# A two-layer decoder trunk on one core: layer 0's mixer with the norm's sums earlier, another order of products, table loads in the planner, and a gate by tanh

## The chip, the cores and the metric

The kernel runs on one core of a Trainium2 chip. A core has five engines, each with its own queue that it works through in order: TensorE (PE; its weight loads are listed as PEld), VectorE (DVE), ScalarE (ACT), GpSimd (POOL) and SyncE (SP), which here only issues transfers. The metric is the device time of one execution in microseconds (us); lower is better. A run's time is that of the whole program; its span goes from the first to the last instruction that the profiler recorded.

## The reference

512 tokens of width 1024 pass through two layers, all in float32. Each layer is a half-step SwiGLU, a mixer and another half-step SwiGLU, each behind an RMS norm. The change lies in the mixer of layer 0:

```
def hybrid_mixer(h, w_in, conv_w, ...):                       # h = rms_norm(x, gain)
    z, xbc, dt_raw, qm, km, vm, om, ig, fg = split_cols(h @ w_in, HY_SPLITS)
    xbc = silu(causal_dwconv(xbc, conv_w, conv_b))            # four taps
    xs, bm, cm = split_cols(xbc, ...)
    y = ssd_chunked(xs, softplus(dt_raw + dt_bias), -exp(a_log), bm, cm, 128) + xs * d_skip
    y = rms_norm(y * silu(z), ssd_norm)                       # in two groups
    hm = mlstm_chunked(qm, km, vm, ig + igate_bias, fg + fgate_bias, 128)
    hm = rms_norm(hm, mlstm_norm) * sigmoid(om)               # the output gate
    return concatenate([y, hm]) @ w_out
```

`ssd_chunked` and `mlstm_chunked` are recurrences over four chunks of 128 tokens, with exponentials of sums of gates.

## The kernel before

**Precision.** Every large product is made of three: a float32 operand is split into a high and a low part ("form"), and high x high, high x low and low x high are added up (`mm3`, lines 235 to 237). The high part is a copy on ScalarE, the low part a difference on VectorE (`parts`, L355 and L357). A form that the code calls `summed` is made otherwise: ScalarE writes the negative (L385), a transfer issued by GpSimd adds the raw weights (L386), ScalarE writes the high part (L387). That spares VectorE and loads the DMA.

**Seven products for eight.** A block of the mixer's input product (512 columns of the weights, called a unit here) is computed by a Strassen-like scheme: seven products of quarters, named A11, A12, A22, S1 to S4 after the form of the features that they use, each 8 x 3 = 24 matrix instructions of 256 columns. Differences of weights are made on VectorE (`less`, L350 on 1024 elements). `product_seven` issues the seven; three of the accumulator banks (tag "hm", four in turn) take them: A holds A11, S2, S3 and A22, B holds A12, D holds S1 and S4. Between two products in one bank the running sum is read out by ScalarE (`keep`, L778) or VectorE (`c11` to `c22`, L350 and L821).

**The mixer's order.** `hybrid` lays down: a small product for the gates (`gates`), which then also issues the norm's sums of squares and reciprocal roots (`settle_later`, twice: L321 on TensorE, a VectorE step L618, a power on GpSimd L620; then L330 on TensorE and a copy on ScalarE L624 that makes the row "rrow") and some fifty tiny operations on the gates; a first unit without the scheme (`unit_eight`, 96 instructions of 512 columns), which needs no scaled features because it is scaled after; the features' seven forms (`xforms`, L438, L350, L355, L357), which need "rrow"; then the units X0, X1 (with a four-tap convolution each, L1034), Z0, Z1, Q, K, V0, V1, O0, O1; the SSD (`ssd`), its gating (`gated`), the mLSTM (`mlstm`) and the output product. The output gate's sigmoid is applied to "og" by ScalarE as O0 and O1 are read out (L824 and L831), and multiplied in L1399. SSD, gating and mLSTM need Exp and Silu on ScalarE.

**What sets the order.** Nothing is issued as it is written. `Plan.add` records each step with its engine, an estimated time, and what it reads and writes; `Plan.order` then schedules the whole program as a list: at each point the step that can start first goes next, among equals the one with the smallest due time (the longest estimated way to the end). TensorE's steps keep their written order within each of several streams ("filler", "ssd", "mlstm"). Buffers are limited by `BUFS` and the `bufs` of each tile: four weight forms in the mixer, four raw weight blocks, two "hu" tiles (the output of the first unit and of X0 and X1, which the convolution reads). The estimate of a ScalarE step knows nothing of function tables, which are loaded (ACT_TABLE_LOAD) when a function needs another table than the one that is in.

## Time and profile before

| | us |
|---|---|
| median of 3 runs | 2032.71 |
| lowest, highest | 2028.99, 2040.58 |
| the profiled execution: its time | 2027.85 |
| its span | 2026.1 |
| TensorE busy in the span | 1963.7 |
| VectorE, ScalarE, GpSimd busy | 1629.9, 1289.5, 321.5 |

In the profile, L12 is line 12 of the kernel; a group is named by its line, engine, operation, and the tiles it writes and reads. A wait is put down to what ended last before it. Busy shares are averages over stages that have different limits, so the mixer, from about 345 to 780 us of the span, is read in stretches. A stretch's granted clock is the share of its full clock that TensorE was given; 0.50 is half speed. The built program has 30 table loads on ScalarE.

### The profile page before, as it was taken

How to read it: one execution, taken by the hardware profiler on the slowest of the kernel's cores; microseconds unless marked ns; L12 is line 12 of the kernel's file. 1: busy time of each engine (PE TensorE's matmuls, PEld its weight loads, DVE VectorE, ACT ScalarE, POOL GpSimd, SP SyncE). 2: the span in 40 equal slices, each digit the busy share in tenths (PEclk: the TensorE clock that was granted, in tenths of full speed). 3: DMA queues.
4: the chain of work that ended last, by engine and by line, in shares of the span. 5: the costliest groups of instructions: out<-in, count | busy, mean ns of one | idle time of the engine just before them, and what ended most of it. 6: DMA issues, size and time to landing. Idle time of an engine off the chain costs nothing.

```text
span 2026.1 us, 36431 instructions
## 1 busy us (share of the span) xinstructions
PE 1963.7 (97%) x14674; PEld 1816.1 (90%) x14674; DVE 1629.9 (80%) x2373; ACT 1289.5 (64%) x1924; POOL 321.5 (16%) x401
## 2 busy tenths in 40 slices
PE   8999999889998999999999999999999999999998
PEld 6999998789997788999999899999966578999998
DVE  6888888798587657989888898979778747988886
ACT  6666666468678753757566566757656834756665
POOL 1000011212124120101012000101323521100010
PEclk9999999999999999999999999999999999999999
DMA  7566666357867442666565366666745202566664
GB/s 219 136 163 154 163 161 166 104 148 180 208 178 218 106 118 64 155 158 167 146 166 149 87 161 173 159 158 157 192 105 103 65 1 84 141 164 160 161 164 118
DMA packets 226609, 292.89 MB, mean 145 GB/s; under 512 B 15036, under 2 KB 196488, under 8 KB 225928
## 3 DMA queue, kind: packets, MB, share of 16 engines
q1 hardware_dynamic: 200728, 199.30, 31.7%
q0 software_dynamic: 25632, 91.24, 24.2%
q8 instruction: 115, 1.88, 0.4%
q14 instruction: 54, 0.44, 0.1%
q10 hardware_dynamic: 80, 0.02, 0.0%
HBM read 192.96 MB, written 6.33 MB: 98 GB/s over the span
## 4 chain that ended last, share of the span: by engine, by line
PE 62%; DVE 6%; ACT 5%; DMA 4%; issue 4%; POOL 1%; ACTq 0%; POOLq 0%; DVEq 0%; SPq 0%
PE pA L236 7%; PE pA L235 7%; PE pA L237 7%; PE pD L235 3%; PE pD L237 3%; PE pD L236 3%; PE hm L235 3%; PE hm L236 3%; PE hm L237 3%; DMA form<-raw 2%; PE pB L235 2%; PE pB L237 2%; PE pB L236 2%; DMA raw<-in_ffn_w_gate 1%; DVE raw L350 1%
## 5 line engine op out<-in xcount | busy, mean ns | idle before, releaser
L357 DVE TENSOR_TENSOR form<-raw,form 128x1024 fp32r<-128x1024 f32 (+2 forms) x382 | 456.3, 1199 | 119.8 <-ACT form L355 118.5
L355 ACT ACTIVATE form<-raw 128x1024 fp32r<-128x1024 f32 (+1 forms) x382 | 392.1, 1030 | 208.2 <-DVE raw L350 138.0
L386 POOL DMA_DIRECT2D form<-raw x172 | 150.9, 879 | 1370.7 <-ACT form L385 1325.2
L350 DVE TENSOR_TENSOR raw<-raw 128x1024 f32<-128x1024 f32 (+2 forms) x281 | 333.1, 1190 | 27.3 <-DMA raw<-in_ffn_w_up 10.7
L235 PE MATMUL pA<-xf,form 128*128 128x256 f32 x1152 | 321.3, 279 | 0.0
L237 PE MATMUL pA<-xf,form 128*128 128x256 f32 x1152 | 320.8, 278 | 0.0
L236 PE MATMUL pA<-xf,form 128*128 128x256 f32 x1152 | 320.7, 278 | 0.0
L385 ACT ACTIVATE form<-raw 128x1024 fp32r<-128x1024 f32 (+1 forms) x172 | 178.1, 1036 | 164.0 <-PE pD L237 70.9
L235 PEld LDWEIGHTS pA<-xf,form 128*128 128x128 f32 x1152 | 217.2, 189 | 0.4
L237 PEld LDWEIGHTS pA<-xf,form 128*128 128x128 f32 x1152 | 217.3, 189 | 0.0
L236 PEld LDWEIGHTS pA<-xf,form 128*128 128x128 f32 x1152 | 217.0, 188 | 0.2
L236 PE MATMUL pA<-hid,form 128*128 128x256 f32 x704 | 198.1, 281 | 4.0 <-DVE hid L357 4.0
L235 PE MATMUL pA<-hid,form 128*128 128x256 f32 x704 | 198.2, 282 | 1.0 <-ACT hid L355 0.9
L237 PE MATMUL pA<-hid,form 128*128 128x256 f32 x704 | 197.0, 280 | 0.0
L387 ACT ACTIVATE form<-raw 128x1024 fp32r<-128x1024 f32 (+1 forms) x172 | 176.3, 1027 | 0.0
L235 PE MATMUL pD<-xf,form 128*128 128x256 f32 x576 | 160.3, 278 | 0.0
L237 PE MATMUL pD<-xf,form 128*128 128x256 f32 x576 | 160.2, 278 | 0.0
L236 PE MATMUL pD<-xf,form 128*128 128x256 f32 x576 | 160.2, 278 | 0.0
L350 DVE TENSOR_TENSOR ft<-ft 128x256 f32<-128x256 f32 (+2 forms) x296 | 151.9, 544 | 5.4 <-ACT ft L604 1.9
L236 PEld LDWEIGHTS pA<-hid,form 128*128 128x128 f32 x704 | 132.4, 188 | 6.0 <-DVE hid L357 6.0
L235 PEld LDWEIGHTS pA<-hid,form 128*128 128x128 f32 x704 | 132.6, 188 | 2.3 <-ACT hid L355 1.5
L237 PEld LDWEIGHTS pA<-hid,form 128*128 128x128 f32 x704 | 132.6, 188 | 0.0
(447 smaller groups left out, 5397.5 us busy)
## 6 DMA issues: line engine op xcount, KB each, us to landing
form<-raw POOLq DMA_DIRECT2D x156, 512.0 KB, 5.6
raw<-in_ffn_w_gate SPq DMA_DIRECT2D x88, 512.0 KB, 4.1
raw<-in_ffn_w_up SPq DMA_DIRECT2D x88, 512.0 KB, 3.7
raw<-in_ffn_w_down SPq DMA_DIRECT2D x64, 512.0 KB, 4.1
raw<-in_hy_w_in SPq DMA_DIRECT2D x44, 512.0 KB, 4.5
raw<-in_ffn_w_down SPq DMA_DIRECT2D x32, 384.0 KB, 3.5
raw<-in_hy_w_out SPq DMA_DIRECT2D x16, 512.0 KB, 3.5
form<-raw POOLq DMA_DIRECT2D x16, 384.0 KB, 4.5
```

The costliest lines, as they stand in the source:

```text
L235: mm(out, l[0], r[0], start=start, stop=False)
L236: mm(out, l[0], r[1], start=False, stop=False)
L237: mm(out, l[1], r[0], start=False, stop=stop)
L350: (self.p if pool else self.v)(n, lambda: e.tensor_tensor(out(), x(), y(), op=op), reads, writes)
L355: self.s(n, lambda: nc.scalar.activation(hi(), src(), AF.Copy), srck, hik)
L357: n, lambda: nc.vector.tensor_tensor(lo(), src(), hi().bitcast(F32), op=ALU.subtract), srck + hik, lok
L385: self.s(n, lambda: nc.scalar.activation(f()[:, 1], raw, AF.Copy, scale=-1.0), rawk, lok)
L386: self.plan.add("gpsimd", 0.85, lambda: nc.gpsimd.dma_start(f()[:, 1], raw, accum_op=ALU.add), rawk + lok, lok, 5.5)
L387: self.s(n, lambda: nc.scalar.activation(f()[:, 0], raw, AF.Copy), rawk, hik)
```

## The change

Four things; the third is in the planner, which orders the whole program, the others are in layer 0's mixer.

1. The norm's sums and rows are taken out of `gates`, which becomes a generator, and issued in `unit_eight` between its first blocks' products. The gates' tiny operations are recorded after the unit's products.
2. `product_seven` issues A11, S1, S2, A12, S3, S4, A22 in place of A11, A12, S1, S2, S4, S3, A22. In the last eight units the summed forms are A12, S4, A22 in place of A12, S2, S4. "hu" has three buffers for two.
3. The planner keeps the table that is loaded: a step that needs another gets 8 us added to its due time (`PATIENCE`), and, once chosen, 1.28 us to its start (`TABLE`). Steps with Silu, Exp and Sin name their table.
4. The output gate is 0.5 * (1 + tanh(om / 2)): ScalarE applies Tanh with scale 0.5, L1399's product becomes (og + 1) * h, and the 0.5 goes into the row factor of the norm (L1419).

```diff
-    LAG = 0.25
+    LAG, TABLE, PATIENCE = 0.25, 1.28, 8.0
...
-        start, free = [None] * n, {e: 0.0 for e, _ in queue}
+        start, free, loaded = [None] * n, {e: 0.0 for e, _ in queue}, None
+        change = lambda i: self.steps[i][7] not in (None, loaded)
...
-                    c = [(max(free[e], known[i]), due[i] + self.steps[i][6], i) for i in q[:most] if known[i] is not None]
+                    c = [
+                        (max(free[e], known[i]), due[i] + self.steps[i][6] + self.PATIENCE * change(i), i)
+                        for i in q[:most] if known[i] is not None
+                    ]
...
-            free[e] = t + self.steps[i][1]
+            if change(i):
+                loaded, start[i] = self.steps[i][7], t + self.TABLE
+            free[e] = start[i] + self.steps[i][1]
...
         keep(kept[0], A)
         self.part_done = [len(self.plan.steps) - 1]
-        B = self.bank("hm")
-        mul(B, b21, self.A12, True)
-        c11(pairs, B)
         D = self.bank("hm")
         mul(D, less(b11, b12, b11), self.S1, True)
         keep(kept[2], D)
         mul(A, less(t2, b22, b11), self.S2, False)
         keep(kept[1], A)
+        B = self.bank("hm")
+        mul(B, b21, self.A12, True)
+        c11(pairs, B)
+        mul(A, less(b12, b22, b12), self.S3, False)
+        c22(pairs, A)
         mul(D, b22, self.S4, False)
         c12(pairs, D)
-        mul(A, less(b12, b22, b12), self.S3, False)
-        c22(pairs, A)
         mul(A, less(t2, b21, t2), self.A22, False)
         c21(pairs, A)
...
                 if func:
-                    self.s(T, lambda: act(o(), o(), func), ok, ok)
+                    self.s(T, lambda: act(o(), o(), func, scale=0.5), ok, ok)
...
         for qs in ((0, 1), (3, 2)):
             for i in range(4):
+                if i in (1, 2):
+                    self.settle_later()
...
-        self.gates(w, g)
+        gates = self.gates(w, g)
+        next(gates)
...
-        self.conv(self.unit_eight(self.columns(w, X0 + 1024), "hu", 2), 8, bc)
+        u = self.unit_eight(self.columns(w, X0 + 1024), "hu", 3)
+        next(gates)
+        self.conv(u, 8, bc)
...
-        many = dict(summed=(self.A12, self.S2, self.S4))
+        many = dict(summed=(self.A12, self.S4, self.A22))
...
-        og = rows(O0, "og", 256, AF.Sigmoid)
+        og = rows(O0, "og", 256, AF.Tanh)
...
+        yield
         plan.stream = "ssd"
-        self.settle_later()
-        self.settle_later()
...
-                self.v(256, lambda ps=ps, h=h, c=c: tt(ox(c, h), ox(c, h), ps()[:, 0:256], op=ALU.mult), [psk, ok(c, h)], [ok(c, h)])
+                self.v(256, lambda ps=ps, h=h, c=c: nc.vector.scalar_tensor_tensor(
+                    ox(c, h), ox(c, h), 1.0, ps()[:, 0:256], op0=ALU.add, op1=ALU.mult), [psk, ok(c, h)], [ok(c, h)])
```

How the built order moves, in three places. The changed kernel's lines are numbered 6 higher up to its `unit_eight`, and 11 higher from the convolution on. First VectorE from the norm's step on the sums (L618, now L624) to the first forms of weights, before:

```order
L618 TENSOR_SCALAR raw<-pssq 128x4
L350 TENSOR_TENSOR raw<-raw 128x1024 x3
L438 SCALAR_TENSOR_TENSOR ft<-raw 128x2x256 x4
L350 TENSOR_TENSOR ft<-ft 128x512 x2
L357 TENSOR_TENSOR xf<-ft,xf 128x512 x2
L350 TENSOR_TENSOR ft<-ft 128x512 x2
L357 TENSOR_TENSOR xf<-ft,xf 128x512
L438 SCALAR_TENSOR_TENSOR ft<-raw 128x2x256 x2
L350 TENSOR_TENSOR hu<-hm,raw 128x512
```

and now:

```order
L624 TENSOR_SCALAR raw<-pssq 128x4
L444 SCALAR_TENSOR_TENSOR ft<-raw 128x2x256 x4
L356 TENSOR_TENSOR ft<-ft 128x512 x2
L363 TENSOR_TENSOR xf<-ft,xf 128x512 x2
L356 TENSOR_TENSOR ft<-ft 128x512 x2
L363 TENSOR_TENSOR xf<-ft,xf 128x512
L444 SCALAR_TENSOR_TENSOR ft<-raw 128x2x256 x2
L356 TENSOR_TENSOR hu<-hm,raw 128x512
L363 TENSOR_TENSOR form<-raw,form 128x1024
L356 TENSOR_TENSOR raw<-raw 128x1024
L363 TENSOR_TENSOR xf<-ft,xf 128x512 x5
```

The three differences of weights that stood ahead of the features' forms now stand among and behind them. On TensorE the sums follow 12 of the unit's 96 instructions in place of 60, and the rows follow 12 later as before.

Second, ScalarE from the last squares (L663, now L669) to the first forms, before:

```order
L663 ACTIVATE ssq<-raw 128x512 x3
L355 ACTIVATE form<-raw 128x1024
L663 ACTIVATE ssq<-raw 128x512
L1020 ACT_TABLE_LOAD
L1020 ACTIVATE raw<-raw 128x16
L355 ACTIVATE form<-raw 128x1024
L385 ACTIVATE form<-raw 128x1024
L624 ACTIVATE raw<-prow 128x512
L387 ACTIVATE form<-raw 128x1024
L355 ACTIVATE form<-raw 128x1024
L355 ACTIVATE xf<-ft 128x512 x5
```

and now:

```order
L669 ACTIVATE ssq<-raw 128x512 x2
L361 ACTIVATE form<-raw 128x1024 x2
L669 ACTIVATE ssq<-raw 128x512
L1031 ACT_TABLE_LOAD
L1031 ACTIVATE raw<-raw 128x16
L630 ACTIVATE raw<-prow 128x512
L361 ACTIVATE xf<-ft 128x512 x7
L361 ACTIVATE form<-raw 128x1024
L361 ACTIVATE xf<-ft 128x512
```

Two weight forms in place of one stand ahead of the last square, and none of X0's ahead of the row and the first seven features' forms.

Third, ScalarE while O0 and O1 are read out beside the SSD's exponentials, before:

```order
L824 ACT_TABLE_LOAD
L824 ACTIVATE og<-og 128x2x256
L1283 ACT_TABLE_LOAD
L1283 ACTIVATE rw<-rw,raw 128x128 x4
L1276 ACTIVATE ce<-rw 128x512
L385 ACTIVATE form<-raw 128x1024
L831 ACT_TABLE_LOAD
L831 ACTIVATE og<-hm 128x2x256
L1283 ACT_TABLE_LOAD
L1283 ACTIVATE rw<-rw,raw 128x128 x4
L387 ACTIVATE form<-raw 128x1024
L824 ACT_TABLE_LOAD
```

and now:

```order
L830 ACTIVATE og<-og 128x2x256
L1287 ACTIVATE ce<-rw 128x512
L830 ACTIVATE og<-og 128x2x256
L1294 ACTIVATE rw<-rw,raw 128x128 x4
L361 ACTIVATE form<-raw 128x1024
L391 ACTIVATE form<-raw 128x1024
L837 ACTIVATE og<-hm 128x2x256
L1287 ACTIVATE ce<-rw 128x512
L393 ACTIVATE form<-raw 128x1024
L1294 ACTIVATE rw<-rw,raw 128x128 x4
```

Tanh and Exp alternate without a load. In all, the built program has 12 table loads in place of 30, and none from the SSD's first exponentials to the next feed-forward stage. The SSD's first transposes (L1231, now L1242) follow the units' products two units later than before; from the end of O1 on TensorE's order is the same.

More of the change, by code (lines that the diff above doesn't have):

```diff
@@ L74, in __init__, with add @@
         self.tail, self.stream, self.later, self.floor = tail or {}, None, 0.0, None
-    def add(self, engine, us, issue, reads=(), writes=(), landing=0.0, after=()):
+    def add(self, engine, us, issue, reads=(), writes=(), landing=0.0, after=(), table=None):
         n, before = len(self.steps), set(after)
@@ L93, in add @@
             before.add(self.floor)
-        self.steps.append((engine, us, issue, before, landing, engine == "tensor" and self.stream, self.later))
+        self.steps.append((engine, us, issue, before, landing, engine == "tensor" and self.stream, self.later, table))
     def lag(self, i, j):
@@ L336, in v, with s @@
         self.plan.add("vector", 0.15 + 1.05e-3 * n, issue, reads, writes)
-    def s(self, n, issue, reads, writes):
-        self.plan.add("scalar", 0.12 + 0.92e-3 * n, issue, reads, writes)
+    def s(self, n, issue, reads, writes, table=None):
+        self.plan.add("scalar", 0.12 + 0.92e-3 * n, issue, reads, writes, table=table)
     def p(self, n, issue, reads, writes):
@@ L830, in last @@
             o, ok = d(0, 1)
-            self.s(T, lambda: act(o(), pairs(bank), func or AF.Copy, scale=scale), [psk], ok)
+            self.s(T, lambda: act(o(), pairs(bank), func or AF.Copy, scale=0.5 if func else scale), [psk], ok)
         self.product_seven(
@@ L1036, in conv @@
                 ), xk + [ak, "par2"], [ak])
-            self.s(T, lambda o=o, acc=acc: nc.scalar.activation(o(), acc(), AF.Silu), [ak], [(*ok, b) for b in range(NB)])
+            self.s(T, lambda o=o, acc=acc: nc.scalar.activation(o(), acc(), AF.Silu), [ak], [(*ok, b) for b in range(NB)], AF.Silu)
     def gated(self, xs, hid, free):
@@ L1123, in gates @@
         vv = lambda n, issue, wr, rd: self.v(n, issue, G(rd), G(wr))
-        ss = lambda n, issue, wr, rd: self.s(n + 100, issue, G(rd), G(wr))
+        ss = lambda n, issue, wr, rd: self.s(n + 100, issue, G(rd), G(wr), AF.Exp)
         tt, ts, stt = nc.vector.tensor_tensor, nc.vector.tensor_scalar, nc.vector.scalar_tensor_tensor
@@ L1207, in gates @@
         plan.stream = "filler"
+        yield
     def spread(self, src, srck):
@@ L1283, in decays @@
                 self.plan.add("scalar", 0.35, lambda j=j: act(e()[:, j], e()[:, j], AF.Exp, bias=nacs()[:, c, 4 * q + j : 4 * q + j + 1]),
-                              [ek, nk], [ek])
+                              [ek, nk], [ek], table=AF.Exp)
             cb, cbk = inner[c]
@@ L1360, in weights @@
                 for h in range(4):
-                    plan.add("scalar", 0.35, lambda h=h: act(qs()[:, h], e()[:, h], AF.Exp, scale=-1.0, bias=ms()[:, c, h : h + 1]), [ek, msk], [qsk])
+                    plan.add("scalar", 0.35, lambda h=h: act(qs()[:, h], e()[:, h], AF.Exp, scale=-1.0, bias=ms()[:, c, h : h + 1]), [ek, msk], [qsk], table=AF.Exp)
                 for h in range(4):
@@ L1367, in weights @@
             for h in range(4):
-                plan.add("scalar", 0.35, lambda h=h: act(e()[:, h], e()[:, h], AF.Exp, scale=-1.0, bias=u()[:, c, h : h + 1]), [ek, uk], [ek])
+                plan.add("scalar", 0.35, lambda h=h: act(e()[:, h], e()[:, h], AF.Exp, scale=-1.0, bias=u()[:, c, h : h + 1]), [ek, uk], [ek], table=AF.Exp)
             ps, psk = self.bank("hc")
@@ L1418, in mlstm @@
             self.p(400, lambda r=r: nc.gpsimd.tensor_tensor(r(), r(), self.mhalf, op=ALU.pow), [part(3)], [part(3)])
-            v4(lambda rd=rd, r=r: tt(r(), r(), rd(), op=ALU.mult), [part(2), part(3)], [part(3)])
+            v4(lambda rd=rd, r=r: nc.vector.scalar_tensor_tensor(r(), rd(), 0.5, r(), op0=ALU.mult, op1=ALU.mult), [part(2), part(3)], [part(3)])
             for h in range(4):
@@ L1481, in rope_tables @@
                 self.s(128, lambda i=i, half=half, src=src: nc.scalar.activation(tab(i)[:, :, half], src, AF.Sin),
-                       ["angs"], [part(i), ("raw", "sum")])
+                       ["angs"], [part(i), ("raw", "sum")], AF.Silu)
         for i, gk in enumerate(("qgain", "kgain")):
@@ L1790, in weights @@
                         accum_out=sm()[:, par, i : i + 1],
-                    ), [(*sk, "n"), (*pk, i), rk], [(*pk, i), (*sk, "s", par)])
+                    ), [(*sk, "n"), (*pk, i), rk], [(*pk, i), (*sk, "s", par)], table=AF.Exp)
                 self.v(4, lambda par=par: v.reciprocal(rs()[:, par], sm()[:, par]), [(*sk, "s", par)], [(*sk, "r", par)])
```

14 lines of the change are left out of this document (7 added, 7 removed).

## The prediction

> **What bounds the kernel now.** I read the page's first part, then the busy time by stretches of layer 0's mixer, then TensorE's waits in it, then the order of time around the largest. TensorE has almost no room outside the waits:
>
> ```profile
> PE 1963.7 (97%) x14674; PEld 1816.1 (90%) x14674; DVE 1629.9 (80%) x2373; ACT 1289.5 (64%) x1924; POOL 321.5 (16%) x401
> ```
>
> So 62.4 us of the 2026.1 us span are open on TensorE (2026.1 - 1963.7), and only a shorter wait, or a higher clock, can shorten the run. The next view cuts the mixer at the first product of each unit: the unit of eight products, X0, X1, Z0, Z1, Q, K, V0, one stretch for V1, then O1 and the first part of the output product. Columns: stretch, its length, busy us of PE, PEld, DVE, ACT, POOL, granted clock, DMA share, GB/s.
>
> ```profile
> 356.74:387.36 30.62, 25.56 (x125) 21.02 (x124) 17.36 (x24) 13.10 (x18) 3.55 (x4) 0.98 0.28 72
> 387.36:413.93 26.57, 22.90 (x169) 22.30 (x170) 24.74 (x33) 12.11 (x16) 9.19 (x6) 0.89 0.49 119
> 413.93:437.59 23.66, 20.58 (x170) 19.97 (x169) 23.52 (x27) 15.69 (x19) 3.33 (x4) 1.00 0.53 135
> 437.59:459.70 22.11, 20.51 (x175) 20.00 (x173) 19.09 (x27) 17.13 (x21) 4.18 (x5) 1.00 0.68 167
> 459.70:480.91 21.21, 20.57 (x176) 20.34 (x174) 20.32 (x39) 15.47 (x21) 4.16 (x5) 1.00 0.72 176
> 480.91:506.09 25.18, 22.58 (x176) 21.98 (x175) 17.97 (x26) 24.70 (x38) 6.79 (x8) 0.93 0.76 199
> 506.09:529.30 23.21, 20.76 (x176) 20.23 (x175) 14.37 (x20) 14.20 (x17) 2.56 (x3) 1.00 0.80 206
> 529.30:549.42 20.12, 19.66 (x173) 19.42 (x172) 12.30 (x19) 14.00 (x20) 2.60 (x3) 1.00 0.79 203
> 549.42:579.79 30.37, 30.37 (x271) 27.59 (x269) 24.00 (x37) 20.63 (x39) 7.49 (x9) 1.00 0.68 179
> 609.89:647.88 37.99, 32.24 (x270) 29.12 (x268) 30.96 (x45) 31.20 (x52) 19.09 (x15) 0.96 0.82 241
> 647.88:700.00 52.12, 48.62 (x221) 40.05 (x222) 33.27 (x74) 42.84 (x94) 8.60 (x9) 0.97 0.46 122
> ```
>
> Seven units of the same 168 products take from 20.12 to 26.57 us. V0, which waits for next to nothing, is the yardstick: a unit is worth 20.1 us. From 549 to 610 TensorE is full and nothing can be won. What the long units wait for (engine and tile waited for; total, times, longest):
>
> ```profile
> PE hm L235 <- ACT xf L355: 6.0, 2, 5.1
> PE hm L235 <- DVE hu L350: 3.4, 2, 2.4
> PE hm L235 <- ACT og L778: 3.2, 1, 3.2
> PE hm L235 <- ACT hh L1081: 2.6, 2, 1.5
> PE hm L235 <- DVE raw L350: 2.2, 2, 1.6
> PE hm L235 <- ACT hu L778: 2.0, 1, 2.0
> PE hm L237 <- DMA form<-raw: 1.9, 2, 1.1
> PE hc L1403 <- ACT gev L1396: 1.8, 1, 1.8
> PE hm L235 <- DVE hq L350: 1.7, 1, 1.7
> ```
>
> The first is the wait for the features' forms at X0. The L350 rows are evacuations of a bank: each A22 stands right behind S3 in the same bank, and starts when VectorE has read S3. In time (columns: stretch, length, PE busy, clock, DMA), the first A11 of X0, an ordinary group of 24, and X0's S3 with its wait:
>
> ```profile
> 387.36:392.62 5.26, 5.26 (x25) 0.50 0.00 0
> 416.75:419.58 2.83, 2.83 (x26) 1.00 0.09 12
> 405.69:410.99 5.30, 2.88 (x26) 1.00 0.77 185
> ```
>
> A group is 2.83 us; the one behind the long wait runs at a granted clock of 0.50 and takes 5.26.
>
> **The change, part by part.**
>
> *Sums and rows earlier.* They stand after 60 of the first unit's 96 product instructions, and now after 12:
>
> ```profile
> 370.74 2.73 PE L321 MATMUL pssq<-raw,ssq 128*128 128x1 f32 x24
> 387.36 0.55 PE L235 MATMUL hm<-xf,form 128*128 128x256 f32 x1 [5.06 <-ACT xf L355]
> 377.96 2.74 DVE L438 SCALAR_TENSOR_TENSOR ft<-raw 128x512 f32<-128x512 f32 x4 [0.72 <-ACT raw L624]
> 354.13 3.22 POOL L350 TENSOR_TENSOR ssq<-ssq 128x512 f32<-128x512 f32 x2 [5.91 <-ACT ssq L663]
> 357.72 0.62 ACT L663 ACTIVATE ssq<-raw 128x512 f32<-128x512 f32 x1
> ```
>
> The 60 run from 356.74 to 370.74, 0.233 us each, so the sums start at 356.74 + 12 x 0.233 = 359.5, 11.2 us earlier. They need the squares: ScalarE's last ends at 358.34, GpSimd's at 357.35, 1.2 us ahead. If ScalarE's new order of squares and weight forms puts the last one behind two 1.05 us forms, TensorE waits, with all later products behind the sums in its queue; I charge 0.5, bounds 0 and 2. L438 follows the sums by 377.96 - 370.74 = 7.2 us, so the forms start at 366.7. The first unit ends at 382.0 and X0's first forms were there 9.4 us behind L438 (387.36 - 377.96), now at 376.1. The wait of 5.06 us goes, and with it the half clock (5.26 - 2.83 = 2.4 us, part of X0's length).
>
> What is late next is VectorE. Its prices from 378 to 549:
>
> ```profile
> L357 DVE TENSOR_TENSOR form<-raw,form 128x1024 fp32r<-128x1024 f32 x31 | 37.7, 1220 | 10.3 <-ACT form L355 10.3
> L350 DVE TENSOR_TENSOR raw<-raw 128x1024 f32<-128x1024 f32 x28 | 33.9, 1219 | 4.6 <-DMA form<-raw 2.8 <-DMA raw<-in_hy_w_in 1.5
> L1034 DVE SCALAR_TENSOR_TENSOR acc<-hu,raw,acc 128x511 f32<-128x511 f32 (+2 forms) x36 | 28.3, 819 | 0.1
> L357 DVE TENSOR_TENSOR xf<-ft,xf 128x512 fp32r<-128x512 f32 x14 | 9.1, 685 | 1.8 <-ACT xf L355 1.8
> L350 DVE TENSOR_TENSOR ft<-ft 128x512 f32<-128x512 f32 x8 | 5.9, 744 | 0.1
> L438 DVE SCALAR_TENSOR_TENSOR ft<-raw 128x512 f32<-128x512 f32 x8 | 5.6, 746 | 0.8 <-ACT raw L624 0.7
> ```
>
> Up to X0's last form the new order has all 30 of the feature instructions (20.6 us), five weight forms (6.1), four differences (4.9) and three evacuations of 0.68 (2.0): 33.6 us, from 366.7 to 400.3. TensorE wants that form at 382.0 + 6 x 2.83 = 399.0. I keep 2 us of waits in X0, bounds 1.3 and 5.
>
> *Order of the products, third "hu" buffer.* Between S3 and A22 now stands S4, 2.83 us in another bank; the longest L350 wait was 2.4, so it hides. A11 and S2 come closer (one group between, not two): if the first read of the bank takes ScalarE over 2.8 us, that is late next. The wait of 2.0 for ScalarE's "hu" is in X1, whose tile is the third to use two buffers and can be written only when the first unit's convolution has read it; the third buffer frees it, and the 36 convolution steps (28.3 us) move to Z0 and later, where VectorE has 2 to 9 us a unit to spare. Against 20.1 us: X0 6.5, X1 3.6, Z0 2.0, Z1 1.1, Q 5.1, K 3.1, V0 0, together 21.4, and 5.06 ahead of X0: 26.4.
>
> *Weight forms through the DMA.* Of A12, S2, S4 in the last eight units, S2 now goes through VectorE and A22 through the DMA. The count stays. A form has four slots, so it has three groups (8.5 us) from free slot to use:
>
> ```profile
> L385 ACT ACTIVATE form<-raw 128x1024 fp32r<-128x1024 f32 x19 | 20.1, 1056 | 18.9 <-PE hm L237 12.0 <-DMA raw<-in_hy_w_in 7.0
> form<-raw POOLq DMA_DIRECT2D x19, 512.0 KB, 5.0
> ```
>
> 1.06 + 0.9 for GpSimd's issue + 5.0 = 7.0, so 1.5 us are to spare. The A22 stalls lengthened A12's lead; now all three are tight. Two of these 19 waited so far, 1.9 us in all. I charge 3 us, bounds 0 and 11 (ten waits of 1.1). DMA work in Q and K is 0.76 x 25.18 = 19.1 and 0.80 x 23.21 = 18.6 us of 20.1; I charge 1.5 more.
>
> *Table loads, tanh.* The built program has 12 loads for 30, and none from the SSD's first exponentials to the next feed-forward stage.
>
> ```profile
> 488.23 1.28 ACT L1283 ACT_TABLE_LOAD   x1
> 489.52 0.69 ACT L1283 ACTIVATE rw<-rw,raw 128x128 f32<-128x128 f32 x2
> L824 ACT ACT_TABLE_LOAD x5 | 6.4, 1283 | 0.1
> ```
>
> 18 x 1.28 = 23 us of ScalarE, which is not what full units wait for. It counts where ScalarE releases TensorE: O1 (37.99 - 32.24 = 5.8 us open, and 0.04 of the clock, 1.5) and the next stretch (52.12 - 48.62 = 3.5, and 0.03, 1.6). Of 7.3 I take 5, since 3.2 is one wait for "og" behind table loads and S4 gets three groups of lead; of 5.1 I take 2, bounds 0 and the whole. The gate's 1 + tanh and the row factor's 0.5 ride in a scalar_tensor_tensor that replaces a tensor_tensor; of 512 elements the two cost 746 and 744 ns above, so 0. That Tanh needs no load beside Exp is read from the order.
>
> [...]
>
> *Sum:* 26.4 - 2 - 3 - 1.5 - 0.5 + 5 + 2 = 26.4 us. The feed-forward stages and the attention change by a few neighbouring instructions; X0 is far from them, so 0. The profiled execution took 2027.85 (span 2026.1, 1.75 around it), 4.9 below the median of 2032.71; on its own scale the result is 2001.5. I add half of that distance: **2004**.
>
> **Rivals.** (1) VectorE is the bound in X0 to Z1: it is busy 24.74 of 26.57, 23.52 of 23.66 and 20.32 of 21.21. Against it: its backlog starts 11.2 us earlier, and the convolution can wait. If VectorE alone sets the pace there, these units end earlier by no more than its earlier start, 11.2 us, less three differences (3.7) that it now does ahead of the forms: 7.5 and not the 16.3 of my sum (13.2 + 5.06 - 2). 2004 + 8.8 = 2013; with nothing won after 610, 2020.
> (2) The summed forms decide. With a landing of L us, 19 forms in X0 to V0 each wait L - 6.5. For it: every lead is now tight, and TensorE asks faster while DMA is at 0.8. Against it: V0 ran at 20.12 with a share of 0.79. From L = 8.0 the gain is gone (19 x 1.5 = 29); at 9 it costs 47 for the 3 charged: 2004 + 44 = 2048, slower.
> (3) The clock falls in each unit. One window at half rate is 0.07 of Q's 25.18 us, 1.7 us; in all ten units 17: 2021. Against it: Z1 and V0 change banks at each group and stay at 1.00.
> [...]
> (4) The waits fall as said but as many appear elsewhere, in queues that run in order (squares, first reads of A, the gates' small products that now stand two units later): no change, 2026.
>
> **How the numbers follow.** Forecast 0.70; (1) 0.12; (2) 0.05; (3) 0.04; (4) 0.09. About 0.5% (10 us) is what a measurement tells from no change. Faster by that means under 2022.5: 0.70 + 0.12 + 0.03 = 0.85; same 0.10, slower 0.05. The forecast's own range is 1992 (the two last terms in full, 5.4, and no charge for forms and DMA, 4.5, make 1994; 2.4 less if the runs lie where the profile does) to 2014 (form waits at 11, 8 more, and 2 lost after 610). Up to 2021 the range takes in (1) and (3).
>
> **What would show it.** Right: X0's first product at 382 without a wait; clock 1.00 from 357 to 550; no L350 wait ahead of A22; V0 ends near 526; ScalarE's groups show 12 table loads. Wrong: waits for L357 forms or features over 4 us in X0 (rival 1); "hm <- DMA form" of 10 us or more (rival 2); 0.5 windows without a long wait (rival 3); waits at L327 for the squares, or at the gates' small products (rival 4).

## The result, and the profile after

The changed kernel takes 2007.74 us in the median of 4 runs (2003.96 to 2011.62), beside 2030.85 us (4 runs) for the kernel before: a ratio of 0.988, 95% interval 0.984 to 0.992. The profiled execution took 2003.96 us, with a span of 2002.2. In a later series it took 2011.03 us in the median of 6 runs (2001.95 to 2013.8) beside 2033.49 (11 runs), a ratio of 0.989 (0.9865 to 0.9917). The forecast was 2004, its range 1992 to 2021.

The first part of the page of the changed kernel; columns as before:

```profile
PE 1956.5 (98%) x14674; PEld 1813.3 (91%) x14674; DVE 1627.8 (81%) x2373; ACT 1264.7 (63%) x1906; POOL 325.0 (16%) x401
```

TensorE's open time, in which it is not busy, is 45.7 us (2002.2 - 1956.5), 16.7 less than before. ScalarE is busy 24.8 us less; 18 table loads of 1.283 us are 23.1 of these.

The mixer falls into three stretches, and nearly everything below is read in them: the **first** from the mixer's first product to Z0 (gates, unit of eight, X0, X1), the **second** from Z0's first product to O1's, the **third** from there to the output product's 97th instruction. Line numbers are 6 higher than before up to the unit of eight, and 11 higher from the convolution on. The stretches of the kernel before:

```profile
347.24:437.59 90.35, 75.70 (x490) 66.00 (x488) 75.12 (x93) 46.93 (x62) 19.59 (x15) 0.96 0.46 123
437.59:609.89 172.30, 164.56 (x1415) 156.88 (x1413) 134.92 (x201) 130.60 (x199) 36.64 (x42) 0.99 0.73 186
609.89:683.53 73.64, 64.39 (x414) 55.16 (x413) 55.32 (x94) 62.18 (x111) 24.88 (x21) 0.95 0.69 197
```

and of the changed kernel:

```profile
346.80:425.02 78.22, 73.79 (x490) 64.69 (x488) 68.44 (x87) 44.84 (x59) 15.84 (x11) 0.98 0.49 131
425.02:597.34 172.32, 164.08 (x1414) 156.91 (x1413) 140.22 (x209) 124.57 (x200) 40.30 (x44) 1.00 0.73 186
597.34:660.88 63.54, 60.89 (x415) 53.52 (x413) 54.85 (x94) 47.66 (x97) 27.57 (x22) 0.97 0.83 236
```

The first stretch lost 12.1 us, the third 10.1, and the second, where the products' order was to earn its gain, nothing: 172.30 and 172.32. By unit (same columns; X0, X1, Z0, Z1, Q, K, V0, V1, O1):

```profile
383.07:404.78 21.71, 20.23 (x170) 19.92 (x168) 21.68 (x27) 13.97 (x18) 4.51 (x3) 1.00 0.57 146
404.78:425.02 20.24, 20.05 (x170) 19.84 (x169) 18.99 (x23) 13.39 (x16) 5.81 (x4) 1.00 0.65 157
425.02:446.07 21.05, 20.14 (x171) 19.93 (x170) 16.87 (x20) 14.06 (x18) 4.19 (x5) 1.00 0.73 175
446.07:467.65 21.58, 20.08 (x170) 19.87 (x169) 15.74 (x19) 14.68 (x19) 4.18 (x5) 1.00 0.73 171
467.65:489.68 22.03, 20.61 (x174) 20.24 (x173) 17.28 (x21) 15.21 (x20) 5.03 (x6) 1.00 0.78 191
489.68:510.79 21.11, 20.47 (x175) 20.29 (x173) 19.67 (x42) 15.23 (x18) 3.45 (x4) 1.00 0.79 203
510.79:534.09 23.30, 22.33 (x190) 21.94 (x189) 16.80 (x31) 17.32 (x22) 3.17 (x4) 1.00 0.83 213
534.09:566.44 32.35, 29.99 (x267) 27.17 (x265) 26.89 (x42) 24.53 (x56) 10.50 (x12) 1.00 0.67 181
597.34:631.09 33.75, 31.19 (x271) 28.81 (x269) 32.68 (x47) 27.09 (x46) 19.74 (x16) 0.95 1.00 296
```

X0 starts at 383.07 with no wait, and runs at full clock (1.00). Q and K gain 3.2 and 2.1 us, V0 and V1 lose 3.2 and 2.0, and V0 ends at 534.09, where the prediction had "near 526". With the second stretch cut in two, Z0 to K and V0 to O0, before:

```profile
437.59:529.30 91.71, 84.42 (x695) 82.55 (x694) 71.75 (x109) 71.49 (x96) 17.68 (x21) 0.98 0.74 187
529.30:609.89 80.59, 80.13 (x722) 74.33 (x720) 63.17 (x93) 59.11 (x103) 18.96 (x21) 1.00 0.71 184
```

and in the changed kernel:

```profile
425.02:510.79 85.77, 81.29 (x683) 80.33 (x681) 69.56 (x99) 59.18 (x75) 16.85 (x20) 1.00 0.76 185
510.79:597.34 86.55, 82.79 (x734) 76.58 (x733) 70.66 (x111) 65.39 (x125) 23.45 (x24) 1.00 0.71 186
```

Z0 to K gained 5.9 us, and V0 to O0 gave back 6.0. What TensorE waits for, from the mixer's first product to that 97th (waiter, releaser: total, times, longest):

```profile
PE hc L1308 <- DVE rw L1297: 4.9, 2, 2.6
PE hm L243 <- DMA form<-raw: 4.0, 4, 1.5
PE hc L242 <- DVE xgn L660: 2.1, 2, 1.3
PE hm L242 <- DVE xf L363: 1.5, 1, 1.5
PE hm L242 <- DMA form<-raw: 1.0, 1, 1.0
...
PE hc L1161 <- DVE gb L1157: 0.6, 1, 0.6
```

Of the rows shown before, those for the features' forms (ACT xf), the evacuations ahead of A22 (DVE hu, raw, hq), "og" and "hh" are gone. New are a wait of the SSD's outputs for "rw", 4.9 us, and forms through the DMA, 5.0 us where 1.9 stood.

### The profile page after: what moved, and what is told of

Its sections match the earlier page's. It is cut to its first block, busy times and chain, and to the rows that moved or that the text cites. A ratio compares the mean times of both kernels' runs of the same rounds, so it can differ in the third digit from the quotient of the medians.

```text
span 2002.2 us, 36425 instructions
## 1 busy us (share of the span) xinstructions
PE 1956.5 (98%) x14674; PEld 1813.3 (91%) x14674; DVE 1627.8 (81%) x2373; ACT 1264.7 (63%) x1906; POOL 325.0 (16%) x401
## 4 chain that ended last, share of the span: by engine, by line
PE 76%; DVE 8%; DMA 8%; issue 5%; ACT 1%; POOL 1%; SPq 0%; POOLq 0%; ACTq 0%; DVEq 0%
PE pA L242 9%; PE pA L241 9%; PE pA L243 9%; PE pD L241 5%; PE pD L243 5%; PE pD L242 5%; DMA form<-raw 3%; PE hm L242 2%; PE hm L243 2%; PE hm L241 2%; PE pB L241 2%; PE pB L243 2%; PE pB L242 2%; DMA raw<-in_hy_w_in 2%; DVE raw L356 2%
## 5 line engine op out<-in xcount | busy, mean ns | idle before, releaser
L361 ACT ACTIVATE form<-raw 128x1024 fp32r<-128x1024 f32 (+2 forms) x382 | 392.1, 1030 | 206.0 <-DVE raw L356 142.4
L391 ACT ACTIVATE form<-raw 128x1024 fp32r<-128x1024 f32 (+1 forms) x172 | 178.2, 1037 | 161.6 <-PE pD L243 74.4
L393 ACT ACTIVATE form<-raw 128x1024 fp32r<-128x1024 f32 (+1 forms) x172 | 176.5, 1027 | 0.0
L242 PEld LDWEIGHTS pA<-hid,form 128*128 128x128 f32 x704 | 132.4, 188 | 5.2 <-DVE hid L363 5.1
L241 PEld LDWEIGHTS pA<-hid,form 128*128 128x128 f32 x704 | 132.6, 188 | 1.4 <-ACT hid L361 0.7
L508 ACT ACTIVATE ft<-pA 128x512 f32<-128x512 f32 x120 | 71.5, 595 | 97.7 <-PE pA L243 90.0
```

The lines of the kernel that those rows point to most:

```text
L241: mm(out, l[0], r[0], start=start, stop=False)
L242: mm(out, l[0], r[1], start=False, stop=False)
L361: self.s(n, lambda: nc.scalar.activation(hi(), src(), AF.Copy), srck, hik)
L391: self.s(n, lambda: nc.scalar.activation(f()[:, 1], raw, AF.Copy, scale=-1.0), rawk, lok)
L393: self.s(n, lambda: nc.scalar.activation(f()[:, 0], raw, AF.Copy), rawk, hik)
L508: self.s(T, lambda: nc.scalar.activation(to(), ps()[:, :, 0:H], AF.Copy), [(*psk, 0), (*psk, 1)], tok)
```

## The experiments

Each row is one profiled execution; "time" is that execution's own, "median" stands where there is a series of runs. One execution's total moves by several us, so the single profiles are read by stretch. How far a stretch moves by itself is seen in the two kernels with two profiles each: their sums differ by 7.4 and 0.6 us, single stretches by up to 4.7. Lengths in us; the kernels are told in the sections behind:

| kernel | first | second | third | sum | time | median |
|---|---|---|---|---|---|---|
| before | 90.35 | 172.30 | 73.64 | 336.3 | 2027.85 | 2033.49 |
| changed, first profile | 78.22 | 172.32 | 63.54 | 314.1 | 2003.96 | 2007.74 |
| changed, again | 77.34 | 175.91 | 68.21 | 321.5 | 2013.69 | 2011.03 |
| sums late | 84.99 | 169.10 | 68.07 | 322.2 | 2017.30 | |
| early sums alone | 83.90 | 173.05 | 74.43 | 331.4 | 2022.27 | |
| old order, rest changed | 78.39 | 170.77 | 62.94 | 312.1 | 2003.19 | |
| the same, again | 78.34 | 169.88 | 63.27 | 311.5 | 1998.64 | 1998.64 |
| new order alone | 93.90 | 168.84 | 69.77 | 332.5 | 2028.39 | |
| tables counted at 0 | 76.61 | 173.51 | 64.83 | 315.0 | 2005.02 | |
| Sigmoid | 78.16 | 171.17 | 73.39 | 322.7 | 2013.43 | |
| two hu buffers | 85.82 | 167.37 | 64.93 | 318.1 | 2011.43 | |
| Tanh, counting, buffer alone | 87.10 | 170.43 | 63.22 | 320.8 | 2016.79 | |
| two sums through the DMA | 76.66 | 167.54 | 72.00 | 316.2 | 2017.01 | |
| mixed orders | 78.68 | 168.61 | 67.38 | 314.7 | 2010.89 | |

### The sums, early and late

The changed kernel, with the sums behind the first unit again:

```diff
-                if i in (1, 2):
-                    self.settle_later()
...
+        plan.stream = "ssd"
+        self.settle_later()
+        self.settle_later()
+        plan.stream = "filler"
```

> The changed kernel with one part undone: the sums of squares and the rows made from them stand behind the first unit's products again; order of products, banks, third buffer, table counting and tanh stay. Theory (the prediction's terms add up): X0's first product goes from 383.1 back to about 387 to 388 with its wait of about 5 us for the features' forms, and X0 gets the half clock again (2.4 us); the products of the units behind keep their gain, so the output product starts 5 to 8 us later than the 631.1 of the changed kernel, at 636 to 639. Rival (VectorE's earlier start carries the gain of X0 to Z1 too, the order of products is worth little): VectorE is late in X0 to Z1 as it was before the change, and the output product starts at 643 or later. Second rival (sums placed early only move the wait into the first unit): output product at 631 to 633.

X0 starts at 389.00 behind a wait of 4.6 us for its forms. Waits of TensorE in X0's first 8 us (start, us, engine, line; the wait in brackets):

```profile
389.00 0.52 PE L241 MATMUL hm<-xf,form 128*128 128x256 f32 x1 [4.56 <-ACT xf L361]
...
395.52 0.38 PE L243 MATMUL hm<-xf,form 128*128 128x256 f32 x1 [1.68 <-DVE form L363]
```

The first stretch is 6.8 us longer than in the changed kernel (7.7 beside its second profile), the second is not. That speaks against the rival of VectorE's early start: late sums leave Z0 and what follows no longer than they were (169.1 us for 172.3 and 175.9). X0 starts 1 us later than the theory's 387 to 388, and the output product at 640.8, 2 us above its 639; 4.9 of it arise in O1 (38.7 for 33.75 us), at a granted clock of 0.82 for 0.95, as in the changed kernel's second profile below (38.79 at 0.82).

The opposite, the kernel before with the early sums and the gates' operations behind the unit's products:

```diff
+                if i in (1, 2):
+                    self.settle_later()
...
-        self.gates(w, g)
+        gates = self.gates(w, g)
+        next(gates)
...
+        u = self.unit_eight(self.columns(w, X0 + 1024), "hu", 2)
+        next(gates)
+        self.conv(u, 8, bc)
...
+        yield
         plan.stream = "ssd"
-        self.settle_later()
-        self.settle_later()
...
+        yield
```

> The kernel before with one part added: the sums of squares and the rows made from them stand between the first unit's products, the gates' small products behind that unit; order of products, two buffers, Sigmoid and the schedule's blindness to table loads stay. Theory (terms add up): X0's first product at about 383 instead of 387.4, no half clock in X0, but the waits ahead of A22 (rows PE hm <- DVE) stay in X0 to K; the output product starts 5 to 8 us earlier than the 647.9 of before, at 640 to 643. Rival (VectorE's earlier start carries most of the gain): the waits ahead of A22 shrink too and the output product starts at 636 or earlier.

6.5 us in the first stretch and nothing behind it; the output product at 644.0, 1 us above the theory's 643. X0 starts at 384.47 without a wait of note, and X1 keeps its 2.0 us for "hu". The rival's time (636 or earlier) is out, though its first half came: the waits ahead of A22 shrank too, from 9.3 us to 6.1.

### The order of the products

The changed kernel with the old order and the old three sums:

```diff
+        B = self.bank("hm")
+        mul(B, b21, self.A12, True)
+        c11(pairs, B)
         D = self.bank("hm")
         mul(D, less(b11, b12, b11), self.S1, True)
...
         mul(A, less(t2, b22, b11), self.S2, False)
         keep(kept[1], A)
-        B = self.bank("hm")
-        mul(B, b21, self.A12, True)
-        c11(pairs, B)
+        mul(D, b22, self.S4, False)
+        c12(pairs, D)
         mul(A, less(b12, b22, b12), self.S3, False)
         c22(pairs, A)
-        mul(D, b22, self.S4, False)
-        c12(pairs, D)
...
-        many = dict(summed=(self.A12, self.S4, self.A22))
+        many = dict(summed=(self.A12, self.S2, self.S4))
```

> The changed kernel with the order of the seven products, and the three sums that go through the DMA, as they were before; early sums, third buffer, table counting and tanh stay. Theory (the prediction's terms): X0 at 383 as in the changed kernel; each unit from X0 to K gets a wait of 1 to 2.4 us ahead of A22 for VectorE's read of S3; 6 to 11 us in all from X0 to V0, O1 1 to 3 more, the output product at 638 to 645 instead of 631.1. Rival (order worth nothing once VectorE starts early, the DMA forms and the gates' place decide): output product at 629 to 634, and V0 back near 20.1 us.

The rival came true in its time: the second stretch is 1.6 us shorter than in the changed kernel, not 6 to 11 longer, and the mixer 2.0 us shorter. (Its mixer starts at 352.53 for 346.80, so the output product's start, 634.65, is 628.9 on the changed kernel's scale, just below the rival's 629 to 634. V0 takes 21.4 us, not the 20.1 that the rival had.)

The kernel before with the new order alone, by the same lines the other way round and

```diff
-        many = dict(summed=(self.A12, self.S2, self.S4))
+        many = dict(summed=(self.A12, self.S4, self.A22))
```

> The kernel before with only the order of the seven products changed, and the summed forms of A12, S4 and A22 through the DMA in the last eight units; two buffers, late sums, Sigmoid and unseen table loads stay. Theory (the prediction's terms): X0 at 387.4 with its wait of 5 us; the rows for waits ahead of A22 go, X1 keeps its wait of 2 us for ScalarE's buffer; the output product at 637 to 642 instead of 647.9. Rival (order worth nothing by itself): 646 to 650. Second rival (new DMA waits of 0.9 to 1.5 us at S4 take back what the order wins): rows hm <- DMA form of 5 us or more, output product at 643 to 647.

The output product starts at 647.88, to the hundredth where it started before. That is the first rival's range (646 to 650). The second stretch is 3.5 us shorter and the third 3.9, the first 3.6 longer; in total the 97th product comes 3.4 us earlier, at 680.17. Differences of this size also appear between two profiles of the changed kernel, so a small gain of the order alone is neither shown nor ruled out.

Timed, beside the changed kernel on one chip:

> The changed kernel with the old order of products and the old three sums through the DMA, timed in five rounds beside the changed kernel and the kernel before on one chip. Theory (the order of the products gains nothing beside the other parts): median within 4 us of the changed kernel, 2000 to 2010, ratio to before 0.984 to 0.990. Rival (the one profiled execution had few half-clock windows by chance and the order is worth the 6 to 11 us of the prediction's terms): 2011 or more. Theory of a gain (its mixer is 2 us shorter): 2000 to 2004.

> The changed kernel itself again, in five rounds beside the run above. 2004 to 2010, ratio to before 0.985 to 0.991, if its first four runs (2003.96 to 2011.62) tell its spread. Measure from the mixer's first product to the 97th product of the output product: 314.1 in its first profile; within 2 us of that if the mixer's length is a matter of the kernel, and more than 3 us off if single half-clock windows move it.

The old order with the other parts takes 1998.64 us (1996.13 to 2008.41), a ratio to before of 0.9846 (0.9820 to 0.9873); the changed kernel's is 0.9891 (0.9865 to 0.9917). Both medians missed what was expected: the first lies below all three ranges given, 12.4 us from the changed kernel and not within 4, and the second 1 us above its 2004 to 2010. The ratios are inside what was expected (0.984 to 0.990 and 0.985 to 0.991). The intervals touch by 0.0008: that the new order costs about 9 us (0.0045 of 2033) is likely, and that it gains 6 or more is out. This is the fastest of the versions that have a series. Its waits, where the changed kernel's stand above:

```profile
PE hm L241 <- DVE raw L356: 3.5, 2, 2.7
PE hc L242 <- DVE xgn L660: 2.0, 2, 1.3
PE hm L241 <- DVE hu L356: 1.9, 2, 1.3
PE hm L241 <- ACT hr L1081: 1.0, 1, 1.0
PE hm L243 <- DMA form<-raw: 1.0, 1, 1.0
...
PE hm L241 <- DVE hq L827: 0.4, 1, 0.4
```

The waits ahead of A22 are there (DVE raw, hu, hq: 5.8 us), but they had been 9.3 in the kernel before (rows hu, raw, hq and hv), and either of the other parts brings them down without any change of order: to 6.1 with the early sums alone, to 5.8 with Tanh, counting and buffer alone. With the new order they go, and 5.0 us for forms and 4.9 for "rw" stand in their place.

**Forms.** Transfers of summed forms in the second stretch: of the kernel before, then of the changed kernel (count, KB, median us from issue to landing):

```profile
form<-raw POOLq DMA_DIRECT2D x21, 512.0 KB, 5.5
```

```profile
form<-raw POOLq DMA_DIRECT2D x21, 512.0 KB, 7.5
```

As many transfers take 2.0 us longer where A22 is summed in place of S2, and this holds in every profile of the two kinds: the seven with the new order and its three sums have 7.0 to 7.8, the five with the old order 4.7 to 5.6. What lengthens them the runs don't show.

**The rw wait in V1.** In the changed kernel, SyncE's queue, then VectorE and TensorE (start, us):

```profile
521.46 0.86 SPq L1174 DMA_DIRECT2D grow<-gr  x1
529.72 0.34 SPq L1224 DMA_DIRECT2D rw<-grow  x1
530.16 0.39 SPq L372 DMA_DIRECT2D raw<-in_hy_w_in  x1
...
535.23 1.23 DVE L356 TENSOR_TENSOR raw<-raw 128x1024 f32<-128x1024 f32 x1 [2.31 <-DMA raw<-in_hy_w_in]
536.37 1.12 DVE L1297 TENSOR_TENSOR rw<-rw,xd 128x512 f32<-128x512 f32 x1
...
537.64 0.62 PE L1308 MATMUL hc<-rw,xd 128*64 128x128 f32 x7 [2.36 <-DVE rw L1297]
```

and what SyncE waited for in V0:

```profile
SPq L1224 <- DMA grow<-gr: 7.3, 1, 7.3
```

The gates' rows go to memory and come back spread over partitions ("grow", then "rw"). The read back waits 7.3 us at the head of SyncE's queue for the copy to land, and a block of weights stands behind it; VectorE waits 2.3 us for that block, "rw" stands behind VectorE's difference, and TensorE waits behind "rw". The planner put the gates' chain later with the new order: its first copy starts at 478.3 before, at 473.1 with the early sums alone and at 491 to 499 with the old order beside the other parts, but at 517 to 535 with the new one, except with two hu buffers (490.5). Of the seven profiles in which it starts behind 520, the one of the mixed orders (below) escapes, where the read back starts 2.3 us later; the other six, two of them of the changed kernel, wait 0.96 to 2.99 us in V1. With an earlier copy no profile waits there over 0.2 us. So the late chain and the wait go together, while the path through the queue is read from this one trace. Why the planner puts the chain later, the runs don't show.

With the old order and the rest changed, the copy, the read back, and VectorE's first use:

```profile
491.15 0.63 SPq L1174 DMA_DIRECT2D grow<-gr  x1
...
495.46 2.80 SPq L1224 DMA_DIRECT2D rw<-grow  x3
...
535.21 0.68 DVE L1297 TENSOR_TENSOR rw<-rw,xd 128x512 f32<-128x512 f32 x1
```

The read back starts 40 us ahead of its use.

**The rw wait in O1.** In the changed kernel, VectorE and GpSimd:

```profile
613.13 2.22 DVE L1297 TENSOR_TENSOR rw<-rw,xd 128x512 f32<-128x512 f32 x1
...
613.23 3.25 POOL L356 TENSOR_TENSOR hss<-hss,hsq 128x512 f32<-128x512 f32 x2
```

The instruction that takes 0.68 us alone takes 2.22 beside two sums of GpSimd, and TensorE waits 2.56 us behind it. A wait for "rw" of 2.07 us or more stands in O1 in all seven profiles with the new order and its three sums, and in none with the old order. What the wait costs differs between two executions of the one program. O1 of the changed kernel's second profile, and the part of it behind this wait:

```profile
601.44:640.23 38.79, 35.96 (x271) 33.27 (x269) 31.42 (x47) 26.85 (x45) 17.92 (x16) 0.82 0.93 262
...
620.70:634.34 13.64, 13.03 (x67) 12.48 (x67) 8.41 (x15) 4.57 (x6) 3.85 (x4) 0.50 1.03 306
```

Behind a wait of 2.07 us there TensorE ran 13.6 us at half clock (0.50); in the first profile, behind 2.56 us, it was

```profile
615.24:618.64 3.40, 3.24 (x22) 2.91 (x23) 3.40 (x4) 1.99 (x3) 2.05 (x2) 0.51 1.04 333
```

3.4 us (0.51). That alone is 5.1 us of time (half of the difference of 10.2). So what was expected of the repeated profile came in its last clause, more than 3 us off: 321.5 against 314.1. Of the 7.4 us, 1.2 are open time of TensorE; the rest is busy time, and the granted clock is lower in the second and third stretches (0.98 and 0.90 for 1.00 and 0.97).

### Tables, Tanh, buffer

The changed kernel, with the planner's numbers at 0:

```diff
-    LAG, TABLE, PATIENCE = 0.25, 1.28, 8.0
+    LAG, TABLE, PATIENCE = 0.25, 0.0, 0.0
```

> The changed kernel, with the schedule's two numbers for table loads (1.28 us for a load, 8 us of patience) set to 0: Tanh, early sums, new order and third buffer stay. The built program has 10 table loads against 12. Measure: from the mixer's first product to the 97th product of the output product, 336.3 us before and 314.1 us in the changed kernel. Theory (Tanh alone takes the loads away; the counting has nothing left to do): 312 to 316. Rival (the patience keeps ScalarE's feature work ahead and the counting earns part of the gain): 317 or more. Second rival (the patience delays the gates' and the SSD's exponentials, so that the SSD's products wait for rw, 4.9 us in the changed kernel): those two waits go and the measure is 308 to 311.

315.0, inside the theory's 312 to 316: Tanh alone takes the loads away (10 are left), and the counting is worth nothing that a single profile could tell (the changed kernel itself had 314.1 and 321.5). The second rival fell: the waits for "rw" stay, 5.1 us.

Sigmoid again, all else changed:

```diff
-                    self.s(T, lambda: act(o(), o(), func, scale=0.5), ok, ok)
+                    self.s(T, lambda: act(o(), o(), func), ok, ok)
...
-        og = rows(O0, "og", 256, AF.Tanh)
+        og = rows(O0, "og", 256, AF.Sigmoid)
...
-                self.v(256, lambda ps=ps, h=h, c=c: nc.vector.scalar_tensor_tensor(
-                    ox(c, h), ox(c, h), 1.0, ps()[:, 0:256], op0=ALU.add, op1=ALU.mult), [psk, ok(c, h)], [ok(c, h)])
+                self.v(256, lambda ps=ps, h=h, c=c: tt(ox(c, h), ox(c, h), ps()[:, 0:256], op=ALU.mult), [psk, ok(c, h)], [ok(c, h)])
...
```

> The changed kernel with the output gate by Sigmoid again, without the 1 + tanh and the factor of 0.5; the schedule still counts table loads. The built program has 24 table loads against 12. Measure as above (314.1 us in the changed kernel). Theory (the gain of the stretches O1 and output product is ScalarE's, and Tanh takes its loads away): O1 gets a wait for og behind table loads of 2 to 5 us and half clock, 319 to 323. Rival (ScalarE's loads lie where TensorE does not wait for it): 312 to 316.

The sum, 322.7, is inside the theory's 319 to 323, but the changed kernel's second profile has 321.5, so O1 and the third stretch have to tell. O1 and its waits:

```profile
597.91:639.39 41.48, 31.90 (x270) 29.12 (x269) 32.83 (x46) 33.25 (x53) 19.08 (x17) 0.92 0.89 251
...
604.86 0.38 PE L241 MATMUL hm<-form,xf 128*128 128x256 f32 x1 [2.24 <-ACT og L837]
...
623.51 0.70 PE L1308 MATMUL hc<-rw,xd 128*64 128x128 f32 x4 [6.68 <-DVE rw L1297]
```

9.6 us of O1 are open (41.48 - 31.90) where the changed kernel has 2.6 and 2.8. The wait for "og" is there, as said, but the larger one is for "rw". In the third stretch, the four kernels with Sigmoid need 69.8 to 74.4 us, those with Tanh 62.9 to 68.2 but for one of the attempts below (72.0).

The parts that are neither sums nor order, as edits of the kernel before. The gates' tiny operations stand behind the first unit here too, as in the changed kernel:

```diff
-    LAG = 0.25
+    LAG, TABLE, PATIENCE = 0.25, 1.28, 8.0
...
-            self.conv(feat(X0 + u * T, "hu", 2, summed=(self.A12, self.S4)), 4 * u, xs[4 * u : 4 * u + 4])
+            self.conv(feat(X0 + u * T, "hu", 3, summed=(self.A12, self.S4)), 4 * u, xs[4 * u : 4 * u + 4])
...
-        og = rows(O0, "og", 256, AF.Sigmoid)
+        og = rows(O0, "og", 256, AF.Tanh)
...
```

> The kernel before with Tanh, the counting of table loads and the third buffer alone: order of products, sums that go through the DMA, and place of the sums of squares as before. Measure as above (336.3 before, 314.1 changed). Theory after the runs so far (the order is worth nothing beside the rest, the early sums 8 us beside the rest and 5 alone): 320 to 324, so that Tanh, counting and buffer carry 12 to 16 of the 22 us. The prediction's own terms (5 of 7.3 in O1, 2 of 5.1 in the stretch behind, 2 for the buffer) give 9: 327. Rival (the parts only gain together: late sums leave VectorE behind, and the loads saved are not what is waited for): 330 or more.

320.8, inside the theory's 320 to 324, where the prediction's own terms gave 327: 3.3 us in the first stretch (X1 takes 20.67 us for 23.66), 1.9 in the second, 10.4 in the third. Early sums on top (the old order above) take another 8.7 and 8.8 us off the first stretch.

Two buffers:

```diff
-        u = self.unit_eight(self.columns(w, X0 + 1024), "hu", 3)
+        u = self.unit_eight(self.columns(w, X0 + 1024), "hu", 2)
...
-            self.conv(feat(X0 + u * T, "hu", 3, summed=(self.A12, self.S4)), 4 * u, xs[4 * u : 4 * u + 4])
+            self.conv(feat(X0 + u * T, "hu", 2, summed=(self.A12, self.S4)), 4 * u, xs[4 * u : 4 * u + 4])
```

> The changed kernel with two buffers for the features ahead of the convolution instead of three; all else stays. Measure: from the mixer's first product to the 97th product of the output product (336.3 us before, 314.1 changed). Theory (X1 waits again 2 to 3 us for ScalarE's write of hu, with a half clock of 1.7 to 3.4 us, and nothing behind it is later): 316 to 319. Rival (the wait of 2 us falls into VectorE's and DMA's slack of the units behind): 313 to 315.

X1, and its longest wait:

```profile
404.83:433.28 28.45, 23.61 (x170) 22.90 (x169) 27.08 (x31) 16.73 (x20) 7.57 (x6) 0.88 0.44 112
...
417.51 0.39 PE L241 MATMUL hm<-xf,form 128*128 128x256 f32 x1 [3.10 <-ACT hu L784]
```

The third buffer is worth 7.6 to 8.5 us of the first stretch, where the prediction had 2.0; about 3.4 of X1's 28.45 us went to the lower clock (0.12 of it). That is its worth under the new order. Beside the old one, Tanh, counting and buffer together take only 3.3 us off the first stretch with late sums, and 5.5 with early ones (83.90 to 78.39). The sum is inside the theory's 316 to 319. But with two buffers the second stretch is 5 us shorter than in the changed kernel's first profile, and V1 has no wait for "rw"; the sum lies between the changed kernel's two, so what the buffer gives in all stays open for the new order.

### Two attempts to keep both gains

A22's sum on VectorE:

```diff
-        many = dict(summed=(self.A12, self.S4, self.A22))
+        many = dict(summed=(self.A12, self.S4))
```

> The changed kernel with only two sums of each of the last eight units through the DMA (A12 and S4), A22's sum on VectorE. Measure as above (314.1). Theory (the waits of 0.9 to 1.5 us for DMA forms at S4, five of them, 5.5 us in all, go, and VectorE, 9 of 16 us busy there, has room for eight more sums of 1.22 us): 308 to 311. Rival (VectorE's 1.2 us a unit come back as waits for forms or for rw): 314 to 318.

316.2: the rival's range (314 to 318). The second stretch fell to 167.5, but forms still wait 3.4 us and the third stretch is 72.0, with a new wait:

```profile
PE hc L327 <- POOL hss L356: 4.4, 1, 4.4
```

The new order up to K, the old one from V0:

```diff
+        if tok:
+            B = self.bank("hm")
+            mul(B, b21, self.A12, True)
...
+        else:
+            D = self.bank("hm")
+            mul(D, less(b11, b12, b11), self.S1, True)
...
-        many = dict(summed=(self.A12, self.S4, self.A22))
+        many = dict(summed=(self.A12, self.S4))
...
-                self.seven_into(self.columns(w, c0 + u * T), xf, dest, keys, tok=True, func=func, **many)
+                self.seven_into(self.columns(w, c0 + u * T), xf, dest, keys, tok=True, func=func, summed=(self.A12, self.S2, self.S4))
```

> The changed kernel with the new order of products in the feature units (X0 to K) alone, where A22's sum goes over VectorE, and the old order with its three sums through the DMA (A12, S2, S4) in the row units (V0 to O1). Measure as above (314.1 changed; 312.1 with the old order everywhere). Theory (each order has its waits in other units: the old one 5.8 to 6.4 us ahead of A22 from X0 to K, the new one 4.9 us for rw in V1 and O1 and 4.8 us for DMA forms): both kinds go, 303 to 309. Rival (the gains of single stages are given back at the next wait, since VectorE's queue, the weights' loads or the SSD's chain set the end): 311 to 316.

314.7: the waits for "rw" are gone, others came (forms 4.5 us, "og" 1.6, "hh" 1.7). The rival holds: what a unit gains is given back at the next thing that is late.

## Why the prediction was right, and where it was not

The total was right to 3.7 us (7.0 in the later series), but one of its three large terms was empty. That it came so close is in part luck: the mixer of the first profile gained 22.2 us for the 26.4 of the sum, as the third stretch gave 3 more than forecast where the order gave nothing; the second profile's mixer gained 14.8.

**Sums, X0 and X1: right in the sum, not in its parts.** By its terms the first stretch was to lose 5.06 + 6.5 - 2 - 0.5 + 3.6 = 12.7 us; it lost 12.1 and 13.0. X0's first product came at 383.07 for 382.0. The 2 us kept in X0 were one wait of 1.48 for VectorE's "xf" in S1, not for X0's last form. How it divides was not seen: the buffer, taken for 2.0, carries 7.6 to 8.5 as the last part put in, the sums 6.8 to 8.8. The two overlap, since together they are more than what the stretch lost.

**Order of the products: wrong.** Z0 to K were to gain 11.3, less 3 and 1.5 for forms and DMA: 6.8. The second stretch gained nothing (172.32) or lost 3.6 (175.91). The step that failed is not "the wait goes, since S4 stands between": no wait ahead of A22 is left, and Z0 to K gained 5.9 us, near the 6.8. It is that V0 was the yardstick and V0 to O0 were priced at nothing, as units where "nothing can be won"; they lost 6.0. Of these, 2.7 us are work: small products of the gates and the SSD that had stood among Z0 to K now stand in V0, which has 190 of TensorE's instructions for 173, so a part of what Z0 to K seemed to owe to waits was work that had to go somewhere (of the 11.3 us only 7.3 were open time, 91.71 - 84.42). And 3.3 us are open time, 2.36 of it the wait for "rw" in V1, behind the gates' chain that the planner moved. The charge of 3 us for forms was too small as well, against 5.0, with landings of 7.5 us and not the 5.0 of the row. Also, part of what was booked on the order belonged to the other parts, which alone bring the waits ahead of A22 from 9.3 us to 5.8 or 6.1.

**Tables and Tanh: right in kind, the size open by some us.** Taken: 7. Measured: 10.4 us in the third stretch with the old order, 10.1 and 5.4 with the new one, where the wait for "rw" (2.56 and 2.07 us in O1) and the half clock behind it (3.4 and 13.6 us) take some back. The built program has 12 loads, as read from the order; ScalarE's busy time fell by 24.8 us, near the loads' 23.1 (18 of 1.283 us). The waits for "og" are gone. That the planner must count tables for it did not show: at 0 the mixer took 315.0.

**The rivals.** (1) VectorE does not bound X0 to Z1: of these four units only X0 has a wait for a feature, 1.48 us, under the 4 us of its sign. (2) The summed forms do not decide. The landing came near the rival's, 7.5 us, but its formula does not hold: 19 waits of 1.0 would be 19 us, and there were five, 5.0 us in all. (3) The clock stands at 1.00 in each unit from X0 to O0 of the first profile, so it does not fall with the change of banks; in the second profile V1 has 0.90, behind a wait of 2.99 us. (4) is what happened in the second stretch, at one of the places it named, the small products that now stand later; its price, the whole gain, was too high.

**The weights of the cases.** Faster by over 0.5% is what came. The range, 1992 to 2021, holds both medians.

## What to carry to other kernels

A wait that is removed is worth its length only as far as the next thing in each queue is ready; that lead is read from the built order and from landing times under the new load (7.5 us here), not from the old median (5.5). Where one planner orders everything, a change in one place moves chains far from it, so undo the parts one at a time and compare stretches, not totals: here the new order had no gain that the runs show, the choice of one function (Tanh beside Exp) gave 5 to 10 us, and the early sums 6 to 9. A unit without waits is a yardstick only if it holds the same work as the others: count its instructions. And look at what stands behind a transfer that waits at the head of a queue: here 7.3 us at SyncE stood ahead of 2.31 at VectorE and 2.36 at TensorE.

## What the runs showed of the hardware

**How long the half clock lasts behind one wait differs between executions.** The stretch behind O1's wait ran at half clock for 3.4 us in one execution of a program and for 13.6 in another, four times as long, behind waits of 2.56 and 2.07 us. What sets the length is not shown; at the start of the longer piece TensorE had one further wait, of 0.8 us for a form. The forecast of 1.00 from 357 on missed another 3.4 us at half clock in the first unit (362.6 to 366.0, at 0.50; 0.98 in the first stretch), which the second profile of the same program does not have (1.00 in that stretch). Stages far from the change move as well. From the first to the last norm sums behind the mixer, the changed kernel and the one with two sums through the DMA:

```profile
750.17:1661.16 910.99, 896.61 (x6626) 812.00 (x6624) 745.93 (x1182) 569.03 (x874) 159.04 (x201) 0.99 0.52 133
...
752.74:1675.74 923.00, 907.19 (x6625) 820.82 (x6623) 745.87 (x1182) 568.84 (x874) 158.98 (x201) 0.98 0.52 132
```

The same work on every engine, 12 us apart, 10.6 of it TensorE's busy time. The second is the longest of the fourteen profiles, which have 908.4 to 923.0 us here. But two profiles of one program differ by 0.8 us (the changed kernel, 911.0 and 911.8) and 0.1 (the old order with the rest changed, 908.5 and 908.4), so it is open whether such a difference is chance of the execution or belongs to the program as built. Either way a total of one execution can't tell parts of this size in the mixer.

**VectorE beside GpSimd.** 0.68 us for 512 elements alone, 2.22 beside GpSimd's two sums (2.26 in the second profile). VectorE's instruction starts 0.1 us ahead of GpSimd's (613.13 and 613.23). What makes it longer there is not shown.
